# Cross-attention of a layer kernel: queries projected features-first, smaller pools, and a written order at the end

## The chip, the cores and the metric

The kernel runs on one core of one Trainium2 chip. A core has engines that work side by side, each with its own instruction queue: TensorE (PE in the profile; its weight loads are PEld), VectorE (DVE), ScalarE (ACT), GpSimd (POOL) and SyncE (SP), which here issues the transfers (DMA). The metric is the device time of one execution in microseconds (us), the median of three runs.

## The reference

One layer with model width 1024 over a sequence of 1024 tokens, all in float32: a mixer (forgetting attention, "fox", beside gated linear attention), cross-attention to 256 memory tokens, and an MLP of hidden width 4096. The change lies in cross-attention:

```python
def memory_cross_attention(hn, memn, wq, wkv, q_norm_g, k_norm_g, wo):
    q = rms_norm((hn @ wq).reshape(B, S, XATTN_HEADS, XATTN_HEAD_DIM), q_norm_g)
    k, v = jnp.split(memn @ wkv, 2, axis=-1)
    k = rms_norm(k.reshape(B, M, XATTN_HEADS, XATTN_HEAD_DIM), k_norm_g)
    ...
    s = jnp.einsum('bshd,bmhd->bhsm', q, k).astype(jnp.float32) / math.sqrt(XATTN_HEAD_DIM)
    p = jax.nn.softmax(s, axis=-1)
    o = jnp.einsum('bhsm,bmhd->bshd', p.astype(v.dtype), v).reshape(B, S, D_MODEL)
    return o @ wo
```

It has 4 heads of 256 features. `hn` is the normalised output h of the mixer's projection, and the result is added to h.

## The kernel before, in words

**Products in three parts.** A float32 operand x is split into a high part (ACT copies it to a rounded type: names ending in h) and a low part (DVE subtracts: names ending in l). `gemm` then issues for each k-tile of 128 rows three TensorE products: high·high (L110), high·low (L111), low·high (L112), in the order of its arguments. `wsplit` loads a weight and splits it (raw, then wh by ACT, wl by DVE). `evac_split` splits a result out of its bank (PSUM).

**What sets the order.** The program is written as Python that names tiles out of pools; a scheduler then fixes each engine's queue from the program's priority, the tiles' dependencies and the buffers of the pools. Pools that are opened over the memory of closed ones make their first writers wait for what last used that memory. `tc.issue_after(x)`, a context, keeps the instructions written under it behind x in the order.

**The stages**, by the time of the trace: mixer inputs and gated linear attention up to about 324 us; fox attention to 558, in which `side_work` fills TensorE's spare time with three things, a part of w_out's projection (`out_part(0)`, products mm), keys and values of the memory, and `out_part(1)`; `project_out` to 590, which leaves h features-first (feature on the partition, token along the row) in `self.h`; cross-attention and the first half of wo to 764; the second half of wo to 840; the MLP to the end.

**Start of fox.** The values of the eight heads are made by token tiles, split into tiles qn of the pool stp, and written to memory as vd (L600). Each head reads its values back as va (L725). Scores s (L660, L661, L663) are reduced and exponentiated, normalised by POOL, transposed (tr, L700), split into pth and ptl and multiplied with va (pv, L707 and L708). Side work's raw loads, splits sh/sl and staging t2k come from the pool "side", opened before the pool of fox's result, mixf.

**Cross-attention before** (`xattn`) goes through eight units of a pair of heads (n) and 256 tokens (u). `queries`: for each 128 tokens `split_tile` splits h in one piece of 1024 columns, 24 products make a token-major query of 512 features (stationary operand: h), `head_rstd` squares it (ACT, L144), sums by DVE (L146) and takes the root's inverse on POOL (L129, L130), DVE multiplies (L1000), four transposes (L1003) turn it and `evac_split` splits it into qh and ql. `attend`, one unit behind: per tile 12 products of 256 columns give scores for two heads, DVE takes the maximum (L1019), ACT the exponential (L1025), POOL multiplies by the reciprocal (L1029), four transposes (L1032), a split into th and tl; then values pv in products of 256 columns (stationary operand: the memory's values), split into o, and written to memory as od in pieces of 256 KB (L1043). After that `project_o_first` loads od back as oh and ol, k-tiles in pairs (L872), splits the first half of wo and makes four blocks of 24 products (`o_block`) for the second half of the tokens. The scheduler mixes these blocks with the last unit's `attend`.

## Time and profile before

| | us |
|---|---|
| time, median of 3 runs | 1449.05 |
| lowest and highest run | 1446.41, 1449.14 |
| profiled execution, its own time | 1448.99 |
| its span in the trace | 1446.9 |
| PE busy in the span | 1427.6 (99%), 7068 instructions |
| DVE busy | 945.3 (65%), 1342 instructions |
| ACT busy | 678.4 (47%), 1095 instructions |
| POOL busy | 389.7 (27%), 404 instructions |

In the profile a row names the source line, the engine, the operation and out<-in by the program's tile names without their numbers. A bracket at the end of a row of the timeline is the idle time of the engine just before it and what ended it. A product's duration overlaps that of the next one, so rates are read as distances between starts. PEclk is the granted clock of TensorE as a share of the full one.

### The profile page before, as it was taken

Reading aid. Unit: us, or ns where it says so; the run is one execution under the profiler, and the core shown is the slowest. Engines: PE = TensorE matmul, PEld = TensorE weight load, DVE = VectorE, ACT = ScalarE, POOL = GpSimd, SP = SyncE. Lnnn points to the kernel's source line nnn. Section 1 sums busy time; section 2 is a strip of 40 time slices with the busy share of each in tenths; the row PEclk is TensorE's granted clock in tenths of the full one; section 3 lists DMA queues with packets and bytes.
Section 4 is the critical chain, followed back from the end, with each engine's and each line's share of the span. In section 5 each row is a group of like instructions: output and inputs, shape, how many; then the busy total and the mean of one; then the engine's idle time right before and its main releaser. Section 6 shows DMA issues by size and latency. Waiting matters only on the chain.

```text
span 1446.9 us, 19214 instructions
## 1 busy us (share of the span) xinstructions
PE 1427.6 (99%) x7068; PEld 1189.7 (82%) x7068; DVE 945.3 (65%) x1342; ACT 678.4 (47%) x1095; POOL 389.7 (27%) x404
## 2 busy tenths in 40 slices
PE   9999999998999999999999999999999999999998
PEld 7788788886888887888888888888888888888887
DVE  5366733428788776666654896655556968688797
ACT  3543441336678565454542364445446645335230
POOL 3235423312242223521212300000000552233455
PEclk9999999999999999999999999999999999999999
DMA  8335520268678642412484114444446835336353
GB/s 312 92 76 129 137 71 0 87 164 261 195 217 232 190 138 87 133 59 88 149 273 168 52 59 181 168 175 189 175 175 214 320 120 189 131 126 223 119 194 124
DMA packets 121165, 223.93 MB, mean 155 GB/s; under 512 B 8912, under 2 KB 54512, under 8 KB 118512
## 3 DMA queue, kind: packets, MB, share of 16 engines
q1 hardware_dynamic: 119776, 218.25, 46.5%
q10 hardware_dynamic: 1296, 4.46, 1.0%
q8 instruction: 56, 0.92, 0.3%
q14 instruction: 37, 0.30, 0.1%
HBM read 150.59 MB, written 72.09 MB: 154 GB/s over the span
## 4 chain that ended last, share of the span: by engine, by line
PE 89%; DMA 5%; ACT 2%; DVE 2%; issue 1%; POOL 0%; SPq 0%; DVEq 0%; ACTq 0%; POOLq 0%
PE mm L110 15%; PE mm L111 15%; PE mm L112 15%; PE my L110 7%; PE my L112 7%; PE my L111 7%; PE tr L112 3%; PE tr L111 3%; PE tr L110 3%; PE tr L700 2%; PE pv L708 1%; PE pv L707 1%; PE s L660 1%; PE s L661 1%; DMA ud<-h 1%
## 5 line engine op out<-in xcount | busy, mean ns | idle before, releaser
L110 PE MATMUL my<-x,g 128*128 128x512 f32 x464 | 180.8, 390 | 0.4 <-ACT h L1288 0.3
L111 PE MATMUL my<-x,g 128*128 128x512 f32 x464 | 180.7, 389 | 0.0
L112 PE MATMUL my<-x,g 128*128 128x512 f32 x464 | 180.6, 389 | 0.0
L111 PE MATMUL mm<-wl,xh 128*128 128x512 f32 x320 | 126.4, 396 | 0.3 <-DVE wl L100 0.3
L110 PE MATMUL mm<-wh,xh 128*128 128x512 f32 x320 | 125.9, 396 | 0.4 <-ACT wh L99 0.3
L112 PE MATMUL mm<-wh,xl 128*128 128x512 f32 x320 | 125.7, 393 | 0.0
L1080 ACT ACTIVATE g<-s 128x1024 fp32r<-128x1024 f32 (+1 forms) x72 | 69.1, 963 | 100.7 <-PE my L112 35.6
L1081 DVE TENSOR_TENSOR g<-raw,g 128x512 fp32r<-128x512 f32 (+3 forms) x72 | 69.4, 967 | 70.0 <-ACT g L1080 69.9
L1080 ACT ACTIVATE g<-raw 128x512 fp32r<-128x512 f32 (+3 forms) x72 | 55.5, 773 | 103.3 <-DMA raw<-in_mlp_w_dram 39.3
L110 PEld LDWEIGHTS my<-x,g 128*128 128x128 f32 x464 | 87.1, 188 | 19.3 <-ACT h L1288 0.7
L111 PEld LDWEIGHTS my<-x,g 128*128 128x128 f32 x464 | 87.1, 188 | 18.3 <-DVE x L1081 0.2
L112 PEld LDWEIGHTS my<-x,g 128*128 128x128 f32 x464 | 87.1, 188 | 18.1
L1107 POOL TENSOR_TENSOR s<-raw 128x384 f32<-128x384 f32 (+1 forms) x20 | 26.5, 1323 | 279.0 <-DMA raw<-in_mlp_w_dram 259.6
L671 POOL TENSOR_SCALAR p<-p,rrec 128x128 f32<-128x128 f32 (+3 forms) x64 | 57.7, 904 | 161.4 <-DVE rrec L670 157.0
L1081 DVE TENSOR_TENSOR g<-s,g 128x1024 fp32r<-128x1024 f32 (+1 forms) x72 | 88.8, 1236 | 8.5 <-ACT g L1080 8.5
L1250 DVE TENSOR_TENSOR x<-x 128x1024 fp32r<-128x1024 f32 (+1 forms) x64 | 76.2, 1209 | 16.5 <-ACT x L1249 16.1
L111 PE MATMUL mm<-x,g 128*128 128x512 f32 x220 | 85.7, 390 | 0.0
L110 PE MATMUL mm<-x,g 128*128 128x512 f32 x220 | 85.6, 389 | 0.0
L112 PE MATMUL mm<-x,g 128*128 128x512 f32 x220 | 85.6, 389 | 0.0
L112 PE MATMUL tr<-x,g 128*128 128x512 f32 x212 | 82.5, 389 | 0.0
L110 PE MATMUL tr<-x,g 128*128 128x512 f32 x212 | 82.5, 389 | 0.0
L111 PE MATMUL tr<-x,g 128*128 128x512 f32 x212 | 82.5, 389 | 0.0
(318 smaller groups left out, 3721.6 us busy)
## 6 DMA issues: line engine op xcount, KB each, us to landing
ud<-h SPq DMA_DIRECT2D x32, 768.0 KB, 3.9
x<-ud SPq DMA_DIRECT2D x48, 512.0 KB, 5.5
raw<-in_mlp_w_dram SPq DMA_DIRECT2D x20, 1024.0 KB, 7.6
raw<-in_mlp_w_dram SPq DMA_DIRECT2D x16, 768.0 KB, 5.9
raw<-in_w_in_dram SPq DMA_DIRECT2D x23, 512.0 KB, 6.3
raw<-in_xattn_wkv_dram SPq DMA_DIRECT2D x16, 512.0 KB, 7.4
od<-o SPq DMA_DIRECT2D x32, 256.0 KB, 4.1
ud<-h SPq DMA_DIRECT2D x32, 256.0 KB, 5.0
```

The source lines that it names most:

```text
L110: mm(ps, lh[k], rh[k], start=start and k == 0, stop=False, **kw)
L111: mm(ps, lh[k], rl[k], start=False, stop=False, **kw)
L112: mm(ps, ll[k], rh[k], start=False, stop=stop and k == n - 1, **kw)
L660: nc.tensor.matmul(ps[:, c], qa[:, ts], ka[:, c], start=True, stop=False)
L661: nc.tensor.matmul(ps[:, c], qb[0:68, ts], kb[0:68, c], start=False, stop=not last)
L671: nc.gpsimd.tensor_scalar(p[:, 0:n], p[:, 0:n], rr, 1.0, ALU.mult, ALU.mult)
L700: nc.tensor.transpose(o, pp[i][:, kb * P:(kb + 1) * P], self.ident)
L707: nc.tensor.matmul(pv, va[:, kb, :], th[:, js], start=kb == 0, stop=False)
L1080: a = self.nc.scalar.activation(hi, src, AF.Copy)
L1081: d = self.nc.vector.tensor_tensor(lo, src, f(hi), ALU.subtract)
L1107: eng.tensor_tensor(s[:, 0], raw[:, 3], raw[:, 2], ALU.add)
L1250: nc.vector.tensor_tensor(lo, f(lo), f(hi), ALU.subtract)
```

## The change

`xattn` is rewritten. It has four units of a pair of heads and 512 tokens, in the order (0, first half), (0, second), (1, second), (1, first). `query` makes 128 features of 512 tokens at a time, features-first, with the weight as the stationary operand: 24 products, no transpose of the query. The query is split as it is, without its norm: ACT squares it; after every second one the two squares are added (POOL, for the very last DVE), transposed in four blocks and summed by DVE, and three small steps on POOL give the factor r, which the exponential takes as its scale. `scores` are as many products as before; `values` multiply 512 columns instead of 256. h is split in pieces of 128 features by 512 tokens out of a pool with nine buffers. od is written in 16 pieces; the read back is cut into k-tiles 0 to 3 (pool op0a), asked for in the last unit, and 4 to 7 (op0b), behind the third unit's values, which are issued ahead of the very last query. The second half of wo's conversions is held behind the last squares. At the end the order is written out: last query, two score tiles, wo block 0, the other two score tiles and two transposes, block 1, two transposes, block 2, the last values, block 3.

Around it: the pool mixf is opened ahead of side, and side is closed after fox; `project_out` splits out of a pool of its own ("mf") and leaves the second half's token factors (`h1_factors(1)`) to `xattn`, behind its second query; several pools get `reuse_waits="tile"` (waits on reused memory by tile); the first loads of the MLP's W1 are held behind the last read back of od. `gemm` returns its last instruction.

```diff
@@ -222,14 +223,16 @@
                 with ExitStack() as mm:
                     self.mm_stack = mm
                     self.mixer_inputs()
-                    self.side = self.open(mx, "side")
                     self.mixf = self.T(self.open(mx, "mixf"), [P, NT, 4, P], F32, "mixf")
-                    self.fox()
+                    with ExitStack() as ss:
+                        self.side = self.open(ss, "side")
+                        self.fox()
                 self.mmp = self.open(lst, "mm3", 2, space=PSUM)
                 self.trp = self.open(lst, "tr3", 2, space=PSUM)
                 self.h = self.T(self.open(st, "h", side="right"), [P, KT, S], F32, "h")
+                self.acc1 = self.T(self.open(st, "acc", side="right"), [P, 512], F32, "acc")
                 self.project_out()
             self.xattn()
             with ExitStack() as mx:
...
-            xp = self.open(st, "xp3", 3)
-            self.acc = [self.T(xp, [P, 512], F32, f"acc{i}", bufs=1) for i in range(2)]
+            kw = dict(reuse_waits="tile")
+            fp = self.open(st, "mf", 6, **kw)
+            xp = self.open(st, "xp3", 3, **kw)
...
-                A = self.split_half(self.side, self.mixf, half, 6, range(4))
+                A = self.split_half(fp, self.mixf, half, 6, range(4))
...
+                if half == 0:
+                    self.h1_factors(half)
...
+    def load_o(self, op, half, ks):
+        oh = self.T(op, [P, len(ks), 512], F32R, "oh")
+        ol = self.T(op, [P, len(ks), 512], F32R, "ol")
+        for j in range(0, len(ks), 2):
+            c, k = slice(j, j + 2), slice(ks[j], ks[j] + 2)
+            self.nc.sync.dma_start(f(oh[:, c, :]), self.od[:, 0, half, k, :])
+            end = self.nc.sync.dma_start(f(ol[:, c, :]), self.od[:, 1, half, k, :])
+        for o, t in zip(self.O.setdefault(half, ([], [])), (oh, ol)):
+            o.extend(t[:, j, :] for j in range(len(ks)))
+        return end.ins
...
     def o_block(self, W, n, half, i, ps, out=None):
         c = slice(i * P, (i + 1) * P)
-        self.gemm(ps, *([w[:, c] for w in w_] for w_ in W), *self.O[half])
+        end = self.gemm(ps, *([w[:, c] for w in w_] for w_ in W), *self.O[half])
         h = self.h[:, 4 * n + i, half * 512:(half + 1) * 512]
         self.nc.vector.tensor_tensor(h if out is None else out, ps, h, ALU.add)
-
-    def project_o_first(self):
-
-        self.ost, self.O = ExitStack(), {}
-        self.load_o(self.open(self.ost, "op0", side="right"), 1)
-        self.Wo = self.wsplit(self.wo[:, 0:512], None)
-        for i in range(4):
-            self.o_block(self.Wo, 0, 1, i, self.T(self.mmp, [P, 512], F32, "mm"))
+        return end
...
+            loaded = self.load_o(op1, 0, range(KT))
...
+            with self.tc.issue_after(loaded):
+                self.A = next(self.W1)
...
     def xattn(self):
...
+            op = self.open(self.ost, "op0a", side="right", **kw)
             sst = ExitStack()
+            sp = self.open(sst, "sp", 9, side="right", **kw)
...
+            def split(half, ks):
+                out = []
+                for k in ks:
+                    sh = self.T(sp, [P, 512], F32R, "sh")
+                    sl = self.T(sp, [P, 512], F32R, "sl")
+                    self.evac_split(sh, sl, self.h[:, k, half * 512:(half + 1) * 512])
+                    out.append((sh, sl))
+                return out
+            def query(u, W, A, j):
+                ps = self.T(mmp, [P, 512], F32, "mm")
+                c = slice(j * P, (j + 1) * P)
+                end = self.gemm(ps, *([w[:, c] for w in w_] for w_ in W), *zip(*A))
+                sq = self.T(sqp, [P, 512], F32, "sq")
+                self.sq_in = nc.scalar.activation(sq, ps, AF.Square).ins
+                q = self.T(qp, [P, 2, 512], F32R, "q")
+                self.evac_split(q[:, 0], q[:, 1], ps)
+                Q.setdefault(u, []).append(q)
+                if j % 2 == 0:
+                    self.sq0 = sq
+                    return end
+                eng = nc.vector if u == j == 3 else nc.gpsimd
+                eng.tensor_tensor(sq, sq, self.sq0, ALU.add)
+                tp = self.T(trp, [P, 512], F32, "tr")
+                for t in range(4):
+                    nc.tensor.transpose(tp[:, t * P:(t + 1) * P], sq[:, t * P:(t + 1) * P], self.ident)
+                ss = self.T(self.smallp, [P, 4], F32, "ss4")
+                nc.vector.tensor_reduce(ss, v4(tp), AX.X, ALU.add)
+                nc.gpsimd.tensor_scalar(ss, ss, 1.0 / 256, None, ALU.mult)
+                half = units[u][1]
+                nc.gpsimd.tensor_tensor(ss, ss, self.hev[:, 4 * half:4 * half + 4], ALU.add)
+                if j == 1:
+                    R[u] = self.T(self.smallp, [P, 2, 4], F32, "rq")
+                nc.gpsimd.tensor_tensor(R[u][:, j // 2, :], ss, self.mhalf[:, 0:4], ALU.pow)
+                return end
+            def scores(u, t):
+                kT = KV[units[u][0]][0]
+                ts = slice(t * P, (t + 1) * P)
+                ps = self.T(sps, [P, 512], F32, "s")
                 for h in range(2):
+                    ks = (2 * h, 2 * h + 1)
+                    end = self.gemm(ps[:, h * M:(h + 1) * M], *([Q[u][k][:, i, ts] for k in ks] for i in range(2)),
+                              *([kT[:, i, k, :] for k in ks] for i in range(2)))
+                r = R[u][:, :, t]
+                nm = self.T(self.smallp, [P, 2], F32, "nm2")
+                nc.vector.tensor_reduce(nm, v2(ps), AX.X, ALU.max, negate=True)
+                nc.vector.tensor_tensor(nm, nm, r, ALU.mult)
+                p = self.T(pp, [P, 512], F32, "p", bufs=4)
+                rs = self.T(self.smallp, [P, 2], F32, "rs2")
+                rr = self.T(self.smallp, [P, 2], F32, "rr2")
+                for h in range(2):
+                    c = slice(h * M, (h + 1) * M)
+                    nc.scalar.activation(p[:, c], ps[:, c], AF.Exp, bias=nm[:, h:h + 1], scale=r[:, h:h + 1], accum_out=rs[:, h:h + 1])
...
+            def transposed(u, t, p):
+                ts = slice(t * P, (t + 1) * P)
+                if t == 0:
+                    TH[u] = [self.T(ptp, [P, 4, 512], F32R, n) for n in ("th", "tl")]
...
+            def values(u):
+                n, half = units[u]
+                vm = KV[n][1]
+                th, tl = TH[u]
+                for j in range(4):
+                    pv = self.T(pvp, [P, 512], F32, "pv")
+                    c, ms = slice(j * P, (j + 1) * P), (2 * (j // 2), 2 * (j // 2) + 1)
+                    end = self.gemm(pv, *([vm[:, i, m, c] for m in range(2)] for i in range(2)),
+                              [th[:, m] for m in ms], [tl[:, m] for m in ms])
+                    o = self.T(pp, [P, 2, 512], F32R, "o")
+                    self.evac_split(o[:, 0], o[:, 1], pv)
+                    nc.sync.dma_start(self.od[:, :, half, 4 * n + j, :], f(o))
+                return end
+            units = [(0, 0), (0, 1), (1, 1), (1, 0)]
+            A = []
+            for u, (n, half) in enumerate(units):
+                if u % 2 == 0:
+                    W = self.wsplit(self.wq[:, n * 512:(n + 1) * 512], C_XAT)
+                if u == 0:
+                    memory(0)
+                    A = split(half, range(KT))
+                keep = A
+                for j in range(4):
+                    if j == 3 and u in (0, 2):
+                        A = split(units[u + 1][1], range(1))
+                    if u == j == 3:
+                        with self.tc.issue_after(values(u - 1)):
+                            end = query(u, W, keep, j)
+                        continue
+                    end = query(u, W, keep, j)
+                    if u == 0 and j == 1:
+                        self.h1_factors(1)
+                    if u and j == 0:
+                        if u == 3:
+                            self.load_o(op, 1, range(4))
+                        for t in range(4):
+                            transposed(u - 1, t, scores(u - 1, t)[0])
+                    elif 0 < u < 3 and j == 1:
+                        values(u - 1)
+                        if u == 2:
+                            memory(1)
+                if u in (0, 2):
+                    A = A + split(units[u + 1][1], range(1, KT))
             sst.close()
+            self.load_o(self.open(self.ost, "op0b", side="right", **kw), 1, range(4, KT))
+            W = self.wsplit(self.wo[:, 0:512], None, steps=[(0, 2), (2, 2)])
+            with self.tc.issue_after(self.sq_in):
+                self.Wo = [a + b for a, b in zip(W, self.wsplit(self.wo[:, 0:512], None, steps=[(4, 2), (6, 2)]))]
+            with self.tc.issue_after(end):
+                ps = [scores(3, t) for t in range(2)]
+            end = ps[-1][1]
+            for i in range(4):
+                with self.tc.issue_after(end):
+                    end = self.o_block(self.Wo, 0, 1, i, self.T(self.mmp, [P, 512], F32, "mm"))
+                with self.tc.issue_after(end):
+                    if i == 0:
+                        ps += [scores(3, t) for t in range(2, 4)]
+                        end = ps[-1][1]
+                    if i < 2:
+                        for t in (2 * i, 2 * i + 1):
+                            transposed(3, t, ps[t][0])
+                    elif i == 2:
+                        end = values(3)
```

**The first attention products of cross-attention, TensorE.** Names are tile and number: s scores, kT keys, mm a query product, tr a transposed bank. Before:

```order
L110 MATMUL s_6414<-kT_6224,qh_6228 128x256
L111 MATMUL s_6414<-kT_6224,qh_6228 128x256
L112 MATMUL s_6414<-kT_6224,ql_6229 128x256
L1003 MATMUL tr_6313<-ident_75,qn_6304 128x128 x4
L110 MATMUL mm_6371<-wh_6186,sh_6367 128x512
L111 MATMUL mm_6371<-wl_6187,sh_6367 128x512
```

The same place in the change:

```order
L112 MATMUL mm_6339<-sh_6253,wl_6218 128x512
L112 MATMUL s_6472<-kT_6221,q_6284 128x256
L110 MATMUL s_6472<-kT_6221,q_6314 128x256
L1014 MATMUL tr_6318<-ident_75,sq_6312 128x128 x4
L178 MATMUL tr_6329<-ident_75,acc_5814 128x128 x4
L110 MATMUL mm_6373<-sh_6225,wh_6183 128x512
```

Before, each query tile is transposed (L1003); now the pair sums sq are (L1014), and here also the token squares of `h1_factors` (L178), which stood in `project_out`.

**The start of fox, TensorE.** s_599 is the first score tile of the next head, mm_2828 side work's first product of w_out, pv_2858 the first product with va. Before:

```order
L663 LDWEIGHTS identb_93
L663 MATMUL s_599_3141<-maskb_98,identb_93 128x128
L112 MATMUL mm_2828<-sh_2820,wl_2805 128x512
L110 MATMUL mm_2828<-sh_2824,wh_2808 128x512
L111 MATMUL mm_2828<-sl_2825,wh_2808 128x512
L112 MATMUL mm_2828<-sh_2824,wl_2809 128x512
L707 MATMUL pv_2858<-pth_2864,va_2426 128x256
```

In the change:

```order
L664 MATMUL s_599_3141<-ka_2849,qa_2847 128x256
L665 MATMUL s_599_3141<-kb_2850,qb_2848 128x256
L667 LDWEIGHTS identb_93
L667 MATMUL s_599_3141<-maskb_98,identb_93 128x128
L711 MATMUL pv_2858<-pth_2864,va_2426 128x256
L110 MATMUL mm_2828<-sh_2812,wh_2794 128x512
L111 MATMUL mm_2828<-sl_2813,wh_2794 128x512
L712 MATMUL pv_2858<-ptl_2865,va_2426 128x256
```

All twelve products of mm_2828 stood ahead of pv_2858; now all of them stand behind its first product. On SP's queue the last write of vd now stands ahead of the load of w_out, and the load of va third behind it.

**The end of cross-attention, TensorE.** mm_7847 and mm_7873 are wo blocks before, mm_7561 is block 0 in the change; oh is read back from od. Before:

```order
L1032 MATMUL tr_7721<-ident_75,p_7713 128x128 x4
L110 MATMUL s_7728<-kT_6930,qh_7505 128x256
L111 MATMUL s_7728<-kT_6930,qh_7505 128x256
L112 MATMUL s_7728<-kT_6930,ql_7506 128x256
L110 MATMUL mm_7847<-oh_7797,wh_7829 128x512
L110 MATMUL mm_7873<-oh_7797,wh_7829 128x512
L110 MATMUL pv_7659<-th_7597,vm_6932 128x256
```

In the change:

```order
L1014 MATMUL tr_7453<-ident_75,sq_7447 128x128 x4
L112 MATMUL s_7513<-kT_7037,q_7449 128x256
L112 MATMUL s_7537<-kT_7037,q_7449 128x256
L110 MATMUL mm_7561<-oh_7174,wh_7475 128x512
L111 MATMUL mm_7561<-ol_7175,wh_7475 128x512
L112 MATMUL mm_7561<-oh_7174,wl_7476 128x512
```

Before, the first product of two wo blocks that reads the last read-back tile stood right behind the last scores; now block 0, which starts with the tile loaded earlier, runs as a whole of 24 products in that place.

More of the change, by code (lines that the diff above doesn't have):

```diff
@@ L111, in gemm @@
             mm(ps, lh[k], rl[k], start=False, stop=False, **kw)
-            mm(ps, ll[k], rh[k], start=False, stop=stop and k == n - 1, **kw)
+            end = mm(ps, ll[k], rh[k], start=False, stop=stop and k == n - 1, **kw)
+        return end.ins
     def evac_split(self, hi, lo, ps, scale=None):
@@ L861, in project_out @@
                     self.add_squares(xp, h, half, i == 0)
-                c = slice(4 * half, 4 * half + 4)
-                self.token_squares(half, self.hv[:, c])
-                nc.gpsimd.tensor_scalar(self.hev[:, c], self.hv[:, c], EPS, None, ALU.mult)
-                nc.gpsimd.tensor_tensor(self.hr[:, c], self.hv[:, c], self.mhalf[:, 0:4], ALU.pow)
-    def load_o(self, op, half):
-        oh = self.T(op, [P, KT, 512], F32R, "oh")
-        ol = self.T(op, [P, KT, 512], F32R, "ol")
-        for k in (slice(k, k + 2) for k in range(0, KT, 2)):
-            self.nc.sync.dma_start(f(oh[:, k, :]), self.od[:, 0, half, k, :])
-            self.nc.sync.dma_start(f(ol[:, k, :]), self.od[:, 1, half, k, :])
-        self.O[half] = [oh[:, k, :] for k in range(KT)], [ol[:, k, :] for k in range(KT)]
+                if half == 0:
+                    self.h1_factors(half)
@@ new lines, in h1_factors @@
+    def h1_factors(self, half):
+        nc = self.nc
+        c = slice(4 * half, 4 * half + 4)
+        self.token_squares(half, self.hv[:, c])
+        nc.gpsimd.tensor_scalar(self.hev[:, c], self.hv[:, c], EPS, None, ALU.mult)
+        nc.gpsimd.tensor_tensor(self.hr[:, c], self.hv[:, c], self.mhalf[:, 0:4], ALU.pow)
+    def load_o(self, op, half, ks):
[7 more added lines that the diff above has]
+            o.extend(t[:, j, :] for j in range(len(ks)))
+        return end.ins
@@ L897, in project_o_rest @@
         with ExitStack() as st:
-            xp = self.open(st, "xp")
+            xp = self.open(st, "xp", **kw)
             sB = self.T(xp, [P, 2, 512], F32, "sB")
@@ L914, in project_o_rest @@
             self.ost.close()
-            self.acc = [self.T(p, [P, 512], F32, "acc") for p in (self.open(mx, "acc", side="right"), xp)]
+            self.acc = [self.acc1, self.T(xp, [P, 512], F32, "acc")]
             x0 = self.open(mx, "x0", 2, side="right", **kw)
@@ L1046, in xattn @@
-            units = [(0, u) for u in range(4)] + [(1, u) for u in (2, 3, 0, 1)]
-            q = []
-            for i, (n, u) in enumerate(units):
-                if i % 4 == 0:
-                    weights(n)
-                q.append(queries(n, u))
-                if i >= 1:
-                    attend(*units[i - 1], q[i - 1])
-                if i == 4:
-                    kst.close()
-            sst.close()
-            attend(*units[-1], q[-1])
-            self.project_o_first()
+            def split(half, ks):
[6 more added lines that the diff above has]
+                return out
@@ new lines, in scores @@
+            def scores(u, t):
+                kT = KV[units[u][0]][0]
+                ts = slice(t * P, (t + 1) * P)
+                ps = self.T(sps, [P, 512], F32, "s")
+                for h in range(2):
+                    ks = (2 * h, 2 * h + 1)
[11 more added lines that the diff above has]
+                    nc.scalar.activation(p[:, c], ps[:, c], AF.Exp, bias=nm[:, h:h + 1], scale=r[:, h:h + 1], accum_out=rs[:, h:h + 1])
+                nc.vector.reciprocal(rr, rs)
+                for h in range(2):
+                    c = slice(h * M, (h + 1) * M)
+                    nc.gpsimd.tensor_scalar(p[:, c], p[:, c], rr[:, h:h + 1], 1.0, ALU.mult, ALU.mult)
+                return p, end
@@ new lines, in transposed @@
+            def transposed(u, t, p):
+                ts = slice(t * P, (t + 1) * P)
+                if t == 0:
+                    TH[u] = [self.T(ptp, [P, 4, 512], F32R, n) for n in ("th", "tl")]
+                tp = self.T(trp, [P, 512], F32, "tr")
+                for j in range(4):
+                    nc.tensor.transpose(tp[:, j * P:(j + 1) * P], p[:, j * P:(j + 1) * P], self.ident)
+                self.evac_split(*(v[:, :, ts] for v in TH[u]), v4(tp))
+            def values(u):
[11 more added lines that the diff above has]
+                return end
@@ new lines, in xattn @@
+            units = [(0, 0), (0, 1), (1, 1), (1, 0)]
[7 more added lines that the diff above has]
+                keep = A
+                for j in range(4):
+                    if j == 3 and u in (0, 2):
[18 more added lines that the diff above has]
+                    A = A + split(units[u + 1][1], range(1, KT))
```

105 lines of the change are left out of this document (19 added, 86 removed).

## The prediction

> **What bounds the kernel now.** I read the page's busy times and its chain first.
>
> ```profile
> PE 1427.6 (99%) x7068; PEld 1189.7 (82%) x7068; DVE 945.3 (65%) x1342; ACT 678.4 (47%) x1095; POOL 389.7 (27%) x404
> PE 89%; DMA 5%; ACT 2%; DVE 2%; issue 1%; POOL 0%; SPq 0%; DVEq 0%; ACTq 0%; POOLq 0%
> ```
>
> TensorE is busy for 99% of the span and carries 89% of the chain that ended last. So the time moves only by TensorE's own products, or by a wait that TensorE shows. Next the windows by stage: the start of fox attention (326 to 338), its body, its end (539 to 558), cross-attention with the first half of wo (590 to 764), and the second half of wo.
>
> ```profile
> core 0: us, PE busy (x) PEld busy (x) DVE busy (x) ACT busy (x) POOL busy (x), PEclk, DMA share, GB/s
> 326.00:338.00 12.00, 9.14 (x32) 5.78 (x30) 10.45 (x20) 9.15 (x20) 2.48 (x2) 0.72 0.97 336
> 338.00:539.00 201.00, 197.29 (x1174) 167.28 (x1175) 157.57 (x302) 134.20 (x291) 60.53 (x71) 0.99 0.69 201
> 539.00:558.00 19.00, 16.03 (x120) 14.08 (x118) 15.75 (x30) 14.13 (x30) 4.33 (x5) 1.00 0.01 2
> 590.00:764.00 174.00, 172.56 (x1015) 151.93 (x1014) 101.65 (x159) 83.95 (x174) 42.27 (x75) 1.00 0.44 147
> 764.00:840.00 76.00, 76.00 (x339) 62.73 (x338) 53.34 (x68) 26.32 (x33) 18.68 (x13) 1.00 0.22 84
> ```
>
> In cross-attention PE lacks 1.44 us of 174 and runs at full clock; DVE is busy 58%, ACT 48%. The second half of wo has no gap. The one uneasy place is the start of fox: 9.14 busy of 12, clock 0.72. TensorE's waits, longest kinds and those met below:
>
> ```profile
> PE s L660 <- ACT p L668: 2.3, 4, 1.2
> PE mm L110 <- DMA oh<-od: 1.4, 1, 1.4
> PE mm L112 <- DVE wl L93: 1.0, 1, 1.0
> PE pv L707 <- DMA va<-vd: 0.9, 1, 0.9
> ```
>
> Of the 1.44 us in cross-attention, 1.4 is one wait, for attention results read back from memory (oh). Everything else there is products. I therefore price the change in products first, then that wait, then what the changed pools do at the start of fox.
>
> **The change, part by part. (a) Fewer transposes.** Before, each of 16 query tiles turns its four normalised blocks (64 transposes). Now only the pair sums of squares are turned, four blocks for every two query products: 32. This is TensorE early in the stage:
>
> ```profile
> 604.43 0.39 PE L110 MATMUL mm<-wh,sh 128*128 128x512 f32 x1
> ...
> 606.93 0.39 PE L112 MATMUL mm<-wh,sl 128*128 128x512 f32 x1
> 607.15 0.28 PE L110 MATMUL s<-kT,qh 128*128 128x256 f32 x1
> ...
> 608.47 0.28 PE L112 MATMUL s<-kT,ql 128*128 128x256 f32 x1
> 608.59 0.60 PE L1003 MATMUL tr<-ident,qn 128*128 128x128 f32 x4
> 608.94 0.48 PE L110 MATMUL mm<-wh,sh 128*128 128x512 f32 x1
> 609.26 0.39 PE L111 MATMUL mm<-wl,sh 128*128 128x512 f32 x1
> ```
>
> A product's duration (0.39) overlaps the next, so I use distances between starts. From 604.43 to 606.93 lie 11 steps: 0.227 us for 512 columns. From 607.15 to 608.47 lie 11 steps of 256 columns: 0.120 us. The four transposes hold PE for 0.35 (608.59 to 608.94), and the product behind them takes 0.32 in place of 0.227, another 0.09. A group thus costs 0.445 us, and 32 fewer transposes are 8 groups: 8 x 0.445 = **-3.6 us**.
>
> **(b) Values in products twice as wide.**
>
> ```profile
> L1003 PE MATMUL tr<-ident,qn x64: 270/272/276, 601.2 to 729.7; 128*128 128x128 f32 x64
> L110 PE MATMUL pv<-th,vm x64: 277/283/364, 634.9 to 750.6; 128*128 128x256 f32 x64
> ```
>
> Each of the three parts of the split has 64 products of 256 columns, 192 in all, and becomes 96 of 512. Priced by the two distances above: 192 x 0.120 = 23.0 to 96 x 0.227 = 21.8, **-1.2 us**. The count agrees with the order: 128 fewer TensorE instructions, 32 + 96. Query products (384 of 512 columns), scores (192 of 256) and the wo blocks keep number and width.
>
> The Trainium skill (TensorE: Matmul & The Clock Gate, Back-to-back issue gap) puts the isolated distance at N/2.4 + 2.5 ns, so that joining two products would save 2.5 ns and the whole part 0.24 us. The trace gives 2 x 120 - 227 = 13 ns a pair; by the page the estimate would come out 1.0 us later. The trace decides.
>
> **(c) The wait for oh.**
>
> ```profile
> 737.47 0.28 PE L112 MATMUL s<-kT,ql 128*128 128x256 f32 x1
> 739.13 0.73 PE L110 MATMUL mm<-oh,wh 128*128 128x512 f32 x2 [1.38 <-DMA oh<-od]
> ```
> ```profile
> 727.46 7.26 DMA od<-o
> 734.74 4.34 DMA oh<-od
> ```
>
> The results of a unit are written out and read back: 7.26 + 4.34 us in this chain, and PE had run out of other work at 737.6. In the change the first four of the eight k-tiles are loaded long before, and the last four come from a unit whose values now stand ahead of the last query (24 products). Call the end of that query T. What follows on PE is fixed: 24 scores, a group of transposes, then the first wo block, and behind it the scores that need the first softmax done.
>
> ```profile
> L118 DVE TENSOR_TENSOR o<-pv,o 128x512 fp32r<-128x512 f32 x16 | 10.8, 685 | 5.8 <-ACT o L117 5.7
> L117 ACT ACTIVATE o<-pv 128x512 fp32r<-128x512 f32 x16 | 9.4, 598 | 11.1 <-PE pv L112 10.5 <-ACT o L117 0.5
> L1025 ACT ACTIVATE p<-s,nm 128x256 f32<-128x256 f32 x32 | 14.9, 472 | 11.3 <-DVE nm L1019 9.4 <-DVE rr L1026 2.0
> L1025 ACT ACTIVATION_READ_ACCUMULATOR p<-s,nm 128x1 f32 x32 | 6.4, 201 | 0.0
> L1026 DVE RECIPROCAL rr<-rs 128x2 f32<-128x2 f32 x16 | 2.5, 161 | 5.8 <-ACT p L1025 5.6
> ```
> ```profile
> L129 POOL TENSOR_SCALAR rs_v<-ss,hev x16: 265/266/685, 599.1 to 723.7; 128x2 f32<-128x2 f32 x16
> L130 POOL TENSOR_TENSOR rs_r<-rs_v,mhalf x16: 695/702/1031, 599.4 to 724.0; 128x2 f32<-128x2 f32 x16
> ```
> ```profile
> DMA to landing us min/median/max: 2.2/4.8/9.3
> ```
>
> The transfers (last row: those that touch od): values end at T - 24 x 0.227 = T - 5.4; their splitting (0.6 + 0.69) lets the last write go at T - 4.1, it lands at T + 0.7 by the median, or T + 3.2 by the 7.26 above; the load adds 4.3, so T + 5.0 to T + 7.5. PE asks for the last pair of k-tiles after 24 x 0.120 + 0.45 + 18 x 0.227 = T + 7.4.
>
> The softmax: PE wants the first score bank back at 24 x 0.120 + 0.36 + 24 x 0.227 = T + 8.7. Nine DVE operations stand ahead of it in the order (sum of squares, query's low part, four low parts of wo, one reduction of squares, two maxima), from about T + 0.8 (square by ACT, 0.6): 9 x 0.685 = 6.2, T + 7.0; POOL's three small steps for the factor (0.27 + 0.70 + 0.70 behind the reduction) end by then. A multiplication of two columns (the reciprocal of as many took 0.16) and two exponentials of 0.47 + 0.20 end at T + 8.5. Both chains arrive just in time. I leave 0.5 us (bounds 0, and 3 if the writes take the longest landing, 9.3): 0.5 - 1.4 = **-0.9 us**.
>
> **(d) Covered work, at nothing.** DVE loses 16 multiplications of queries and 8 of 16 reductions (about 16 us), ACT little; POOL gains seven additions of squares. All of it lies beside PE's 172 us, and so does the splitting of h in 24 pieces: for a new half 8 x 0.685 = 5.5 us of DVE, freed piece by piece while the last query of the old half runs for 24 x 0.227 = 5.4 us; one spare buffer of nine gives the lead. If cover were gone, that is rival two. The 16 writes of od in place of 32 move the same bytes.
>
> **(e) The start of fox.** The staging pool of the side work now lies where the mixer's staging lay, so the load of w_out and the splits beside it must wait until the last write of the values (vd) has landed; va, which reads vd, is asked for earlier in the queue; and TensorE now stands before va's product with w_out's products (mm) behind it, where these twelve came ahead. Before:
>
> ```profile
> 330.00:336.80 6.80, 5.51 (x15) 3.44 (x14) 6.80 (x14) 4.79 (x10) 2.48 (x2) 0.50 1.06 387
> ```
> ```profile
> 337.45 0.39 PE L112 MATMUL mm<-sh,wl 128*128 128x512 f32 x1
> 338.72 0.39 PE L707 MATMUL pv<-pth,va 128*128 128x256 f32 x1 [0.88 <-DMA va<-vd]
> 339.31 0.38 PE L700 MATMUL tr<-ident,p 128*128 128x128 f32 x2
> ```
> ```profile
> 324.15 0.44 SPq L80 DMA_DIRECT2D raw<-in_w_out_dram  x1
> 325.90 0.53 SPq L600 DMA_DIRECT2D vd<-qn  x1
> 333.23 0.80 SPq L725 DMA_DIRECT2D va<-vd  x2
> ```
>
> vd, issued at 325.9 among other loads, landed at about 333.2, when va was let go; va took 5.5 us. In the change vd goes out alone, so it may land sooner than after 7.3 us; w_out then arrives later, va earlier. PE did twelve products (2.7 us at full clock) and four of va by 339.3, 6.8 us of it at half clock. Above: all the idle and the half clock vanish, 5.51/2 + 1.05 + 0.88 = -4.7. Below: vd lands no sooner, +7.5 (the last rival). A landing some 3 us sooner makes va's product start near 336 and the twelve end near 339, as now. I take **0**.
>
> The Trainium skill (TensorE: Matmul & The Clock Gate, Part 1: The HAM clock gate) says that an idle window of about 3.4 us halves the clock, and as much busy time restores it. By that, TensorE waiting for va from 330 to 336 would start the twelve products at half clock and lose 3.4/2 = 1.7 us, an estimate of 1445.0 for the whole. The trace's half clock held for 6.8 us, 5.5 of them busy, longer than the page's window; it is a loss that the kernel before has too, so the sum doesn't count it again.
>
> **Sum.** The profiled execution took 1448.99 us, its span 1446.9 and 2.1 around it; the median of the runs is 1449.05, the same. 1448.99 - 3.6 - 1.2 - 0.9 + 0 = **1443.3 us**.
>
> **Rivals.** *One: a better start of fox.* If vd's landing alone takes 3 us, PE keeps its clock and (e) is -4.7: 1438.6. For it: DMA share 1.06 in that window, so the landing was slowed by company. Against it: PE still has nothing between its scores and va. *Two: DVE and ACT set the pace in cross-attention.* Two more DVE operations than I count ahead of the needed one, at both changes of half and at the end: 3 x 2 x 0.685 = +4.1, 1447.4. For it: the DVE queue at the end has 0.2 us to spare. Against: 58% busy before, less now. *Three: the wait for oh stays as it was*, because the last write is still followed at once by its load: +0.9, 1444.2. *Four, slower: the start of fox stalls.* vd lands at 333.2; the short queue ahead (0.4 + 0.5 + 0.6) lets va go at 334.7 and arrive at 340.2; PE, idle meanwhile, does va's four (0.6) and then the twelve (2.7), and loses half of 6.8 us to the clock: 346.9 in place of 339.3. That is +7.6, 1450.9. It decides from the point at which va arrives later than about 339. For it: every instruction behind va's product waits too. Against: vd's write without company.
>
> **Chances.** My forecast 0.47, with an own range of 1441 to 1446 (bounds of c); rival one 0.13, two 0.18, three 0.10, four 0.12. A measurement of this kernel can tell about 0.2%, 2.9 us. Faster by more than that (below 1446.1): 0.47 + 0.13 + 0.10 = 0.70; within it 0.18; slower 0.12. The range for 8 in 10 leaves out half of rival one's and most of rival four's cases: 1438.0 to 1449.5.
>
> **What would show it.** In the changed profile: 6940 TensorE instructions; 96 value products 0.227 us apart; cross-attention's window shorter by 5 to 6 us; no oh wait over 0.6 at the first wo block; TensorE's wait for va near 336. A va wait of several us, or waits for exponentials or low parts inside cross-attention, would make the prediction wrong.

## The result

The change makes the kernel slower: 1459.66 us against 1448.99 us (medians of six runs each), a ratio of 1.0076 with a 95% interval of 1.006 to 1.0093. The profiled execution of the change has a span of 1458.0 us, 11.1 more than before.

```profile
span 1458.0 us, 18869 instructions
PE 1424.0 (98%) x6940; PEld 1180.4 (81%) x6940; DVE 938.4 (64%) x1343; ACT 678.7 (47%) x1103; POOL 387.3 (27%) x403
```

TensorE is busy 3.6 us less (1424.0 for 1427.6), with 128 instructions fewer, and the span is longer all the same: it is idle for 34.0 us (1458.0 - 1424.0) where it was for 19.3. Where, two rows tell: the last of the products with va (the end of fox), and the last of wo's products. The source view of their line gives, behind the durations, the first and the last start. Before:

```profile
L708 PE MATMUL pv<-ptl,va x160: 274/283/562, 338.9 to 556.6; 128*128 128x256 f32 x160
L112 PE MATMUL mm<-oh,wl x128: 387/389/478, 728.2 to 829.2; 128*128 128x512 f32 x128
```

The change:

```profile
L712 PE MATMUL pv<-ptl,va x160: 274/283/415, 339.7 to 568.3; 128*128 128x256 f32 x160
L112 PE MATMUL mm<-oh,wl x128: 387/389/476, 739.1 to 840.4; 128*128 128x512 f32 x128
```

Fox ends 11.7 us later. From there to the end of wo it takes 272.1 us in place of 272.6, so the rewritten cross-attention saves 0.5 us and not 5.7. Where in fox the time goes, windows tell (first the length, then PE's busy time): the start from 320 to 345, and the rest up to its end. Before:

```profile
320.00:345.00 25.00, 20.54 (x94) 15.05 (x94) 20.02 (x38) 17.25 (x36) 7.70 (x8) 0.86 0.85 255
345.00:556.60 211.60, 206.07 (x1252) 175.27 (x1251) 165.63 (x314) 143.03 (x307) 60.82 (x73) 0.99 0.62 183
```

The change:

```profile
320.00:345.00 25.00, 16.13 (x80) 12.96 (x79) 16.76 (x32) 14.69 (x32) 5.13 (x7) 0.80 0.72 210
345.00:568.30 223.30, 210.32 (x1272) 177.63 (x1271) 170.86 (x321) 146.76 (x313) 57.89 (x73) 1.00 0.61 183
```

TensorE is busy as long as before (226.5 us for 226.6 in the two windows together). Its idle time grows by 4.4 us at the start (4.5 to 8.9) and by 7.5 behind it (5.5 to 13.0). So the start is the smaller part of the loss. The waits of TensorE in the change, longest first:

```profile
PE pv L711 <- ACT wh L88: 8.5, 1, 8.5
PE s L664 <- ACT p L672: 5.3, 7, 1.7
PE tr L704 <- DVE ptl L119: 3.2, 4, 1.5
PE mm L110 <- ACT t2k L775: 2.4, 2, 1.3
PE pv L110 <- ACT th L118: 1.3, 1, 1.3
PE mm L111 <- DMA ol<-od: 1.1, 2, 0.7
...
PE mm L110 <- DVE h L852: 0.9, 1, 0.9
...
PE pv L110 <- DVE o L119: 0.7, 2, 0.3
```

The first four belong to fox, the others to cross-attention. The first is the start of fox:

```profile
329.77 0.23 PE L667 MATMUL s<-maskb,identb 128*128 128x128 bf16 x1
338.46 0.55 PE L711 MATMUL pv<-pth,va 128*128 128x256 f32 x1 [8.46 <-ACT wh L88]
338.81 0.63 PE L110 MATMUL mm<-sh,wh 128*128 128x512 f32 x1
```

The windows of that idle time and of the stretch behind it (the third number from the end is the granted clock):

```profile
329.80:338.40 8.60, 0.20 (x3) 0.06 (x1) 6.96 (x12) 6.80 (x13) 0.49 (x1) 0.75 0.78 249
338.40:344.00 5.60, 5.54 (x22) 4.96 (x23) 4.28 (x10) 3.40 (x8) 1.47 (x2) 0.50 1.04 298
```

TensorE stands for 8.5 us and then works for 5.6 us at half clock. Half of that, 2.8 us, is lost by an estimate; but the kernel before works 5.51 us at half clock in this place too (its window from 330 to 336.8, shown in the prediction), so the clock is no part of the difference. What is late shows on SP's queue and where ACT converts the weight:

```profile
313.83 12.90 SPq L604 DMA_DIRECT2D vd<-qn  x3
330.05 0.37 SPq L748 DMA_DIRECT2D gxk<-in_xattn_k_norm_g_dram  x1
330.49 0.41 SPq L80 DMA_DIRECT2D raw<-in_w_out_dram  x1
...
331.47 0.44 SPq L729 DMA_DIRECT2D va<-vd  x1
```
```profile
335.69 2.19 ACT L88 ACTIVATE wh<-raw 128x512 fp32r<-128x512 f32 x4 [1.27 <-DMA raw<-in_w_out_dram]
```

The load of w_out went out at 330.49; before, at 324.15. It stood behind the last write of vd, whose data weren't ready before some 326 us, and then behind its landing. So when TensorE ran out of scores at 330, neither va nor w_out was there. (The wait is put down to ACT's wh, of which va's product takes nothing. Its inputs are pth, split by 333.4, and va, whose transfer had been under way since 331.47; of these only va can still have been open at 338. In SP's queue va went out fourth behind the write: after gxk, w_out's load and a t2k.)

### The profile page after: what moved, and what is told of

Same layout as the page of the kernel before. It is cut to its first block, busy times and chain, and to the rows that moved or that the text cites. A ratio compares the mean times of both kernels' runs of the same rounds, so it can differ in the third digit from the quotient of the medians.

```text
span 1458.0 us, 18869 instructions
## 1 busy us (share of the span) xinstructions
PE 1424.0 (98%) x6940; PEld 1180.4 (81%) x6940; DVE 938.4 (64%) x1343; ACT 678.7 (47%) x1103; POOL 387.3 (27%) x403
## 4 chain that ended last, share of the span: by engine, by line
PE 45%; DMA 2%; ACT 2%; DVE 1%; issue 1%; SPq 0%; DVEq 0%; ACTq 0%
PE my L110 7%; PE my L111 7%; PE my L112 7%; PE mm L111 5%; PE mm L112 5%; PE mm L110 5%; PE tr L111 3%; PE tr L112 3%; PE tr L110 3%; DMA ud<-h 1%; DMA raw<-in_mlp_w_dram 1%; DMA ol<-od 1%; ACT x L1146 0%; DMA od<-o 0%; ACT g L1146 0%
## 5 line engine op out<-in xcount | busy, mean ns | idle before, releaser
L110 PE MATMUL mm<-sh,wh 128*128 128x512 f32 x256 | 101.9, 399 | 2.1 <-ACT t2k L775 1.1
L112 PE MATMUL mm<-sh,wl 128*128 128x512 f32 x256 | 100.7, 394 | 0.0
L111 PE MATMUL mm<-sl,wh 128*128 128x512 f32 x256 | 100.7, 394 | 0.0
L675 POOL TENSOR_SCALAR p<-p,rrec 128x128 f32<-128x128 f32 (+3 forms) x64 | 52.8, 832 | 160.6 <-DVE rrec L674 153.6
```

Source lines behind the costliest of these rows:

```text
L110: mm(ps, lh[k], rh[k], start=start and k == 0, stop=False, **kw)
L111: mm(ps, lh[k], rl[k], start=False, stop=False, **kw)
L112: end = mm(ps, ll[k], rh[k], start=False, stop=stop and k == n - 1, **kw)
L675: nc.gpsimd.tensor_scalar(p[:, 0:n], p[:, 0:n], rr, 1.0, ALU.mult, ALU.mult)
```

## The experiments

Each was timed in five or three rounds against the kernel before on the same chip; each time stands with its ratio to that. "Fox ends" is the last start in the row shown above, in the profiled execution. It is good to some 3 us: e5 and e7 to e10 have the same fox, and theirs ends at 555.8, 556.7, 555.6, 553.9 and 556.2.

### The pools and the new cross-attention apart

e1 undoes the pools around fox:

```diff
+                    self.side = self.open(mx, "side")
                     self.mixf = self.T(self.open(mx, "mixf"), [P, NT, 4, P], F32, "mixf")
-                    with ExitStack() as ss:
-                        self.side = self.open(ss, "side")
-                        self.fox()
+                    self.fox()
...
-                A = self.split_half(fp, self.mixf, half, 6, range(4))
+                A = self.split_half(self.side, self.mixf, half, 6, range(4))
```

> The change with the pools of before around fox and project_out (side opened ahead of mixf and kept to the end of project_out, whose splits come out of it again); cross-attention as changed. The order of fox is then that of before. Theory P (the pools cost some 11 us in fox, the new cross-attention is worth about 0.5 us): 1448.5, fox as long as before, cross-attention and wo 272 us as in the change. Rival X (the new cross-attention costs the time, and fox only shows it): 1457 to 1460.

e2 makes the same edit the other way round, in the kernel before.

> The kernel before with only the new pools (mixf ahead of side, side closed after fox, project_out's splits from a pool of their own); cross-attention as before. Theory P: 1460, slower by 11 us, all of it between the start and the end of fox. Rival X: within 1 us of before, 1449.

| | time | ratio, interval | fox ends | from there to wo's end |
|---|---|---|---|---|
| before | 1448.76 | | 556.6 | 272.6 |
| change (its own comparison) | 1459.66 | 1.0076 (1.006 to 1.0093) | 568.3 | 272.1 |
| e1, old pools | 1456.69 | 1.0052 (1.0035 to 1.0069) | 553.4 | 279.3 |
| e2, new pools alone | 1464.66 | 1.011 (1.0094 to 1.0126) | 568.1 | 276.9 |

The ends of fox follow the pools: 568 with the new ones, 553 to 557 with the old. That half of theory P holds. The other half falls: with the old pools the new cross-attention costs 6.7 us instead of saving 0.5, and the whole comes near rival X's 1457, though fox is short. e2, too, is slower by more than theory P's 11 us: by 15.9, of which 4.3 lie behind fox. The reason in e1 is one wait, in e1's timeline of TensorE:

```profile
586.41 0.39 PE L112 MATMUL mm<-sh,wl 128*128 128x512 f32 x1
592.13 1.22 PE L110 MATMUL mm<-sh,wh 128*128 128x512 f32 x2 [5.33 <-ACT sh L118]
```
```profile
592.00:598.60 6.60, 6.11 (x14) 4.32 (x15) 6.37 (x9) 4.24 (x9) 1.11 (x1) 0.51 0.18 68
```

The first query waits 5.3 us for splits of h, and then runs 6.6 us at half clock (3.3 lost, an estimate): 8.6 us together. ACT makes the first of these splits at 591.47, right behind project_out's last squares; in the change it makes the first at 578.55, 24 us ahead of the first query. The two kernels differ in the pools alone, so it is the pools that hold the splits back in e1. So the new pools have a job, memory that is free for these splits, and fox pays for it. And with the pools held fixed the new cross-attention is worth 276.9 - 272.1 = 4.8 us. e1's six runs lie between 1452.1 and 1458.8 us, wider than those of e2 to e4, and the profiled one is the fastest; what the slower ones add isn't in this trace.

### What in the pools costs fox its time

e3 changes how the side pool waits, and nothing in any engine's order:

```diff
-                        self.side = self.open(ss, "side")
+                        self.side = self.open(ss, "side", reuse_waits="tile")
```

> The change with one word more: the side pool waits on reused memory tile by tile. Every engine's order stays that of the change; the load of w_out and the splits beside it no longer wait for the landing of vd. Theory W (these waits make the stall at the start of fox): the idle time ahead of va's product falls from 8.5 to about 5 us and the whole by 3 to 4 us, to 1456. Rival O (the order makes it: TensorE stands before va's product with the twelve products behind it, whenever w_out arrives): idle still over 7 us, 1458 to 1460.

e4 adds an order of work to it:

```diff
-                        values(h, sb, (pp[2 * sb], pp[2 * sb + 1]), A)
+                        if h == sb == 0:
+                            with self.tc.issue_after(self.first_mm):
+                                values(h, sb, (pp[2 * sb], pp[2 * sb + 1]), A)
+                        else:
+                            values(h, sb, (pp[2 * sb], pp[2 * sb + 1]), A)
```

> As the run before, and va's first product is held behind w_out's first product block, so that TensorE does these products while va is under way, as in the kernel before. Rival O: the start of fox loses no more than before, and the time falls by 4 us or more, to 1455 or less. Theory W alone: no better than the run before, 1456. If the whole 11 us of fox follow from its start, 1449.

e3 took 1456.98 us (1.0059, 1.0045 to 1.0073), fox ended at 565.1; the idle time fell from 8.5 to 6.4 us. So the wait for vd's landing was worth 2.7 us by the medians (the two intervals overlap), between the two theories' numbers and nearer to W; most of the loss is something else. Behind 345 TensorE is idle for 12.2 us in e3, nearly as in the change (13.0), with every engine's order as in the change: it is not the wait for the landing that makes the later part. e4 took 1455.52 (1.0048, 1.0035 to 1.0062), fox ended at 563.2: the order is worth another 1.5 us by the medians, less than rival O asked for, and the intervals of e3 and e4 overlap so far that it may be nothing. TensorE now waited 4.9 us for w_out, since its load still went out behind vd's write, at 326.70. What was left was the place of this load.

e5 puts it back, and keeps the free memory for the new splits, with two pools in place of one:

```diff
+                    self.side = self.open(mx, "side")
                     self.mixf = self.T(self.open(mx, "mixf"), [P, NT, 4, P], F32, "mixf")
                     with ExitStack() as ss:
-                        self.side = self.open(ss, "side")
+                        self.up = self.open(ss, "side2", reuse_waits="tile")
...
-            xt = self.T(mp, [P, 4, M], F32, "memr")
+            xt = self.T(self.up, [P, 4, M], F32, "memr")
...
-                kv = self.T(mp, [P, 2, 512], F32R, "mkv", bufs=2)
+                kv = self.T(self.up, [P, 2, 512], F32R, "mkv", bufs=2)
```

> The change with side work's tiles in two pools: splits sh and sl, the gain gxk, w_out's raw tiles and the staging t2k in a pool ahead of mixf that project_out then uses for its splits, memr and mkv in one behind mixf that is closed after fox. The load of w_out stands ahead of the last write of vd again, and the splits of cross-attention have free memory as in the change. Theory Q (the loss in fox comes from tiles that lie over the values' staging and so go behind vd): fox ends at 553 to 557 as with the old pools, cross-attention and wo take 272 us as in the change, 1445 to 1449. Rival (closing side early costs fox its time in itself): 1453 or more.

e6 moves side work's raw tiles, those of w_out and those of wkv, to the upper pool (`rooms=self.up`), and nothing else.

> As the run before, but w_out's raw tiles are in the upper pool (and mkv too), so that the load of w_out stands behind the last write of vd in SP's queue. Theory Q: the idle time before the first products of w_out or va is again 5 us or more, fox ends 4 to 8 us later than in the run before, 1452 or more. Rival (the place of this one load doesn't matter): within 1.5 us of the run before.

| | time | ratio, interval | fox ends | from there to wo's end |
|---|---|---|---|---|
| before | 1448.45 | | 556.6 | 272.6 |
| e5, two pools | 1447.40 | 0.9993 (0.9981 to 1.0004) | 555.8 | 271.8 |
| e6, raw tiles above | 1452.72 | 1.003 (1.0017 to 1.0043) | 561.3 | 270.8 |

SP's queue in e5:

```profile
324.65 0.43 SPq L80 DMA_DIRECT2D raw<-in_w_out_dram  x1
...
326.40 0.52 SPq L605 DMA_DIRECT2D vd<-qn  x1
...
333.26 0.88 SPq L730 DMA_DIRECT2D va<-vd  x2
```

and in e6:

```profile
326.23 0.52 SPq L605 DMA_DIRECT2D vd<-qn  x1
326.82 0.65 SPq L80 DMA_DIRECT2D raw<-in_w_out_dram  x1
```

Theory Q holds in kind. With the load ahead of the write fox is as short as before, and the whole 12 us faster than the change. The place of the raw tiles alone is worth 5.3 us; the longest wait at the start was 2.7 us, not the 5 expected. Most of e6's loss comes later: from 345 to the end of fox TensorE is idle for 4.4 us in e5 and for 10.1 in e6. Some of it lies in waits that the change has too and that are shorter in e5 (e5's view, then e6's, whose first row holds the 2.7 of the start):

```profile
PE s L665 <- ACT p L673: 2.1, 3, 1.2
PE tr L705 <- DVE ptl L119: 1.5, 1, 1.5
```
```profile
PE tr L705 <- DVE ptl L119: 4.1, 4, 2.7
PE s L665 <- ACT p L673: 3.1, 4, 1.3
PE mm L110 <- ACT t2k L776: 2.5, 2, 1.3
```

That the later waits come with the tiles' place is shown. By which of the scheduler's choices, is not; and as the raw tiles of wkv moved along, e6 doesn't show what the one load of w_out is worth by itself.

### The waits in cross-attention

In the change TensorE goes straight from the last transposes to the values that need them:

```profile
720.88 1.03 PE L1056 MATMUL tr<-ident,p 128*128 128x128 f32 x8
723.20 0.73 PE L110 MATMUL pv<-th,vm 128*128 128x512 f32 x2 [1.28 <-ACT th L118]
```

and in wo's first block it waits for the read back:

```profile
742.13 0.50 PE L111 MATMUL mm<-ol,wh 128*128 128x512 f32 x1 [0.32 <-DMA ol<-od]
...
744.71 0.50 PE L111 MATMUL mm<-ol,wh 128*128 128x512 f32 x1 [0.73 <-DMA ol<-od]
```

e7 to e10 start from e5, whose cross-attention has the same waits but for the first of the two for ol, so that 0.7 us is left there. e7 cuts the last query:

```diff
+                if u == j == 3:
+                    end = self.gemm(ps, *(w[:4] for w in L), *(a[:4] for a in R4), stop=False)
+                    with self.tc.issue_after(end):
+                        end = values(u - 1)
+                    with self.tc.issue_after(end):
+                        end = self.gemm(ps, *(w[4:] for w in L), *(a[4:] for a in R4), start=False)
```

> As e5, and the last query product is cut in two: twelve products ahead of the third unit's values, twelve behind. Theory C (values wait for their split th because the written order leaves nothing to put between): the wait of 1.3 us before the values is gone, and the whole is 1 to 1.5 us faster than e5. Rival (the later write of od only moves the wait to the read back): the wait for ol grows by as much, no change within 0.5 us.

It took 1445.80 us (0.9988, 0.9976 to 1.0001). The wait ahead of the values is gone, and at the read back it is there again:

```profile
731.41 0.47 PE L110 MATMUL mm<-oh,wh 128*128 128x512 f32 x1 [1.01 <-DMA oh<-od]
732.65 0.50 PE L111 MATMUL mm<-ol,wh 128*128 128x512 f32 x1 [0.77 <-DMA ol<-od]
```

From the end of fox to wo's end the trace has 271.6 us, e5 271.8: by the trace the rival holds. The median is 1.6 us below e5's, which is what theory C asked for; but the intervals overlap almost whole, and the trace shows no gain in the stage that was changed. e8 halves the bytes to be read back (for the last four k-tiles `ol = oh`, and no load of ol).

> As e5, but the low part of the last four k-tiles of o is not read back: the high part stands in for it in the products, so 1 MB is read instead of 2 MB, with the same products on TensorE (the output lacks that part). Theory B (four loads share the bandwidth, and that makes the wait of 1.05 us for ol): no wait for the read back in wo's first block, about 1.5 us faster than e5. Rival (the landing of od's writes makes it): the same wait, on oh.

It took 1447.29 us (0.9989, 0.9975 to 1.0003), like e5. There is no wait for the read back any more, and another one has come in its place, for the first softmax, at the scores behind wo's first block:

```profile
733.05 0.39 PE L110 MATMUL s<-kT,q 128*128 128x256 f32 x1 [1.41 <-ACT p L1046]
```

The bandwidth theory is right on the wait. On the time e8 decides nothing, because ACT's order moved as well. The bank that these scores want is free when the first two exponentials are done. In e5 the second of them ends ahead of a conversion of wo (wh):

```profile
731.67 0.19 ACT L1043 ACTIVATION_READ_ACCUMULATOR p<-s,nm,rq 128x1 f32 x1
...
733.12 0.63 ACT L88 ACTIVATE wh<-raw 128x512 fp32r<-128x512 f32 x1 [0.16 <-DMA raw<-in_xattn_wo_dram]
```

In e8 this conversion stands ahead of the exponentials and waits for its load:

```profile
731.28 0.63 ACT L88 ACTIVATE wh<-raw 128x512 fp32r<-128x512 f32 x1 [3.40 <-DMA raw<-in_xattn_wo_dram]
...
732.81 0.20 ACT L1046 ACTIVATION_READ_ACCUMULATOR p<-s,nm,rq 128x1 f32 x1
```

So e8's wait of 1.41 us comes from this order. In e5 the softmax was done at 731.86, and its scores, which began at 733.11, would have wanted it at 732.4 without the 0.73 us for ol: 0.5 us to spare. e9 was made in the belief that both chains end too late, and gives both more cover: it cuts the first two wo blocks.

```diff
+            for i in range(2):
+                with self.tc.issue_after(end):
+                    end = self.gemm(bk[i], *L(i, lo), *O(lo), stop=False)
+            with self.tc.issue_after(end):
+                ps += [scores(3, t) for t in range(2, 4)]
+                end = ps[-1][1]
...
+            for i in range(2):
+                with self.tc.issue_after(end):
+                    end = self.gemm(bk[i], *L(i, hi), *O(hi), start=False)
```

> As e5, and the first two wo blocks are cut: their products over k-tiles 0 to 3 come first for both, then the last two score tiles of the fourth unit, then their products over k-tiles 4 to 7. Twelve products (2.7 us) more lie ahead of the first product that needs the late read back, and ahead of the scores that need the softmax. Theory D (read back and softmax end a little too late side by side, so that only cover for both helps): no wait for ol nor for exponentials there, 1 to 1.5 us faster than e5, which leaves the waits ahead of the values (1.3) and at the start (0.9). Rival (the wait moves on once more): within 0.5 us of e5.

> As e9, and the last query cut in two around the third unit's values as in e7. Theory D: the wait ahead of the values is gone too and doesn't come back at the read back; cross-attention and wo take 269 us in place of 271.8, the whole 1444 to 1445, faster than before by some 3 us. Rival: the later write of od takes the gain back, 1446 or more.

e9 took 1444.81 us (0.9975, 0.9961 to 0.9988), e10 1445.25 (0.9982, 0.9969 to 0.9995), the kernel before 1447.38 in these runs. Both are faster than before, by 2.6 and 2.1 us. From the end of fox to wo's end they took 270.4 and 269.3 us: theory D's forecast of the waits holds, that for the read back is gone in both, and e10 has the 269 us that were expected; its time is 0.25 us above the range given. This 1.1 us between them doesn't show in their times, whose intervals overlap. That only cover for both chains helps was not tested: no run gives it to the read back alone. And e9's lead on e5, 2.6 us by medians from two chips, is 1.4 us in the stretch behind fox; fox itself is the same in both. The windows of that stretch, before, in the change, and in e9 (first the length, then PE's busy time):

```profile
557.00:829.50 272.50, 271.06 (x1453) 233.44 (x1452) 166.10 (x244) 114.11 (x221) 75.02 (x98) 1.00 0.40 133
```
```profile
568.40:840.70 272.30, 268.35 (x1327) 224.86 (x1326) 157.85 (x245) 113.87 (x229) 79.65 (x97) 1.00 0.37 130
```
```profile
554.00:824.60 270.60, 267.77 (x1327) 224.88 (x1326) 157.15 (x245) 113.87 (x229) 79.15 (x97) 1.00 0.38 130
```

TensorE's idle time there is 1.4, then 4.0, then 2.8 us, with some 3 us less work in the last two.

## Why the prediction was wrong, step by step

The forecast was 1443.3 in a range that ended at 1449.5; the change took 1459.66. Its sum set against the traces, by distances between starts from the end of fox to wo's end (a gap over 0.4 us above its kind's distance counted as a wait):

| term | predicted | measured |
|---|---|---|
| (a) fewer transposes | -3.6 | -3.6 |
| (b) values twice as wide | -1.2 | -0.5 |
| (c) waits in cross-attention | -0.9 | +3.5 |
| (e) fox | 0 | +11.7 |
| sum | -5.7 | +11.1 |

**(a) was right.** All transposes of this stretch take 11.5 us for 14.1, and the products behind them 1.0 less (queries 121.4 for 121.8, scores 23.6 for 24.3).

**(b) was mis-sized.** The 96 wide products stand 0.236 us apart, not 0.227, which I had from the query products; so a pair saves 5.6 ns, not 13. The Trainium skill (TensorE: Matmul & The Clock Gate, Back-to-back issue gap) would have 2.5 ns by its isolated distance. The measured value lies between that figure and the row I used.

**(c) was wrong in two steps.** I took the landing of the read back from one load's 4.3 us. Four of 512 KB follow each other with two of wo's raw loads ahead of them; the last was issued at 736.67, and the product that waits for it began at 744.71, 8.0 us later. e8, with two of the four left, has no wait there. And (d) priced the cover of the values at nothing: the change itself holds the last query behind the third unit's values, so that nothing lies between their transposes and them (1.3 us), and at the start of the stage DVE has the conversions of wq ahead of project_out's last sums (0.9). Two waits of the values for a free bank (0.7 together) had no term either. The softmax, given as just in time, was: in the change the second exponential was done at 744.72, and without the 1.05 us for ol its bank would have been wanted at 744.92.

**(e) was the step that failed: the start of fox was put at 0, and what the new order does to the rest of fox had no term.** I bounded it by -4.7 and +7.5 and took 0, since vd would land sooner without other loads beside it. It did: issued at about 326.2 it let gxk go at 330.05, 3.9 us later. But va's product then began at 338.46, not near 336. I had va let go at vd's landing and 5.5 us under way; it went out at 331.47, behind gxk, w_out's load and a t2k, and its product began 7.0 us after that. The twelve products of w_out, now behind it, ended at 347, not 339, with some of fox's other products among them. That rival four's end (346.9) agrees is in part luck: it had vd landing at 333.2 and the half clock as a loss, while vd landed early and the half clock was there before too. The start has 4.4 us more idle time in all. The other 7.5 of the 11.9 us come behind 345, in waits for exponentials, for ptl and for t2k; I had looked at the start alone.

What brought both is the pools: e2 has the long fox with the old cross-attention, e1 and e5 have the short one with the new. Within the pools the wait for vd's landing was worth 2.7 us (e3) and the place of side work's raw tiles 5.3 (e6 against e5), most of it in later waits. How the scheduler comes to the order with the later waits stays open. The chance given to a slower kernel, 0.12, rested on an average of two bounds where the order already showed TensorE with nothing between its last score and va.

Rival two's waits on DVE and ACT in cross-attention are in part what (c) measured. Rival one, a better start of fox, did not come.

## What to carry to other kernels

Where a pool moves over memory of a stage that is just ending, look first at what its first tiles load, and where these loads stand in the queue. Then look at the order of the whole stage and not at its start alone: here 7.5 of 11.9 us of added idle time lay behind the start. A new layout can be needed in one stage and harmful in another; splitting one pool in two, with the early loads below and the late tiles above, kept the short fox and the free memory for the splits (e5). Where an edit takes a wait away and another appears, compare the order of every engine before the two are called one behind the other: in e8 a conversion had moved ahead of the exponentials.

## What the runs showed of the hardware

The exponentials became dearer by taking their scale from a tile. In the change's groups of instructions:

```profile
L1043 ACT ACTIVATE p<-s,nm,rq 128x256 f32<-128x256 f32 x32 | 17.7, 562 | 17.6 <-DVE nm L1037 16.5 <-PE s L112 1.1
```

562 ns each for 472 before, of the same shape: 90 ns for the one more operand. The Trainium skill (ScalarE: Activation LUTs, What ACT_TABLE_LOAD costs) gives about 93 ns for each such operand, and this trace agrees. I hadn't counted it; two of them, 0.18 us, stand in the softmax chain of (c).

In the change the granted clock was 0.50 in the 5.6 us of work behind 8.5 us of idle time, in e1 0.51 in the 6.6 us behind 5.3. By an estimate, half of the stretch, that cost 2.8 and 3.3 us beside the waits themselves, and no list of waits shows it. A long idle time isn't needed for it. In e5 the clock goes down behind a wait of 1.24 us and stays down for longer than in either:

```profile
328.70:342.30 13.60, 12.32 (x37) 9.05 (x38) 13.36 (x26) 9.20 (x19) 4.74 (x3) 0.51 1.01 325
```

What sets its length, these runs don't show.
